# The opening of a two-layer backbone kernel, ordered by feature tiles

## Chip, cores and metric

The kernel runs on one core of a Trainium2 chip. The metric is the time of one execution on the device, in microseconds (us); for a kernel it is the median of several runs. A separate execution is recorded by the hardware profiler; from it come the page of the profile and the trace.

The engines of a core: TensorE (PE; its weight loads are shown apart as PEld) does the matrix products, VectorE (DVE) and ScalarE (ACT) work on whole tiles of 128 partitions, GpSimd (POOL) does some more of this, and SyncE (SP) issues transfers from the chip's main memory (DMA).

## The reference

Two layers over 512 latent tokens `x` (1024 features) and 256 context tokens `ctx`, all in float32. Every layer is a mixer and a SwiGLU feed-forward part (FFN), each behind an RMS norm whose result is scaled and shifted ("modulated") by six vectors per stream that are computed from a conditioning vector. Layer 0 mixes by windowed attention with 16 query heads and 4 heads of keys and values, layer 1 by retention. Cut to what bears on the change:

```python
c_act, cc_act = silu(c), silu(c_ctx)
for i in range(2):
    mx = split(c_act @ ada_w[i] + ada_b[i], 6)        # latent: shift, scale, gate, shift, scale, gate
    mc = split(cc_act @ ada_w[i] + ada_b[i], 6)       # context
    h_x = rms_norm(x, norm1_g[i]) * (1 + mx[1]) + mx[0]
    h_c = rms_norm(y_ctx, norm1_g[i]) * (1 + mc[1]) + mc[0]
    # layer 0
    q_x, k_x, v_x = split(h_x @ w_qkv, [1024, 1280])
    k_c, v_c = split(h_c @ w_qkv[:, 1024:], 2)
    q_x, k_x = rope_2d(rms_norm(q_x)), rope_2d(rms_norm(k_x))
    out_x = softmax([q k_c, q k_window, sink]) [v_c, v_window] @ w_o
    # layer 1: retention with decay log_g = log_sigmoid(ret_decay_logit)
    x = x + mx[2] * out_x                             # y_ctx likewise in layer 0
    x = x + mx[5] * swiglu(rms_norm(x) * (1 + mx[4]) + mx[3])
```

## The kernel before

**Layout and precision.** All activations stand with features on the partitions and tokens along the free axis: `x` is eight tiles (one for each 128 features) of 128x512, the context eight of 128x256. A float32 operand of a matrix product is split into a rounded high part and the remainder, and each product is three matmuls, high·high, low·high, high·low (`mm3`, L143). A weight tile of 128x1024 comes by a DMA, ScalarE makes its high part by a copy, VectorE its low part by a subtraction (`split`, L163, or in the opening `split_w` and `split_low`, L380 and L384).

**Order.** Each engine runs its own instructions strictly in order. In the opening that order is the program's own, written out by hand in a block (L469 to L518) for TensorE, VectorE and ScalarE; a second block (L635 to L652) holds TensorE's order up to the context's values, while a scheduler orders the other engines there. After it the scheduler orders all of them. All weights come through the queue of SyncE, in the order in which the program issues them; an issue whose buffer is still in use holds up those behind it. Pools with a fixed number of buffers of a name set how far ahead a load may be ("adan" has eight, "wraw" two).

**The opening**, in the order of its code:

- `load_stream` (L168) loads `x` in eight tiles. `add_square` (L205) squares each tile on ScalarE and adds it on VectorE to one list of sums, seven adds for eight tiles. `rms` (L216) sums this over the partitions by a matmul with a matrix of ones, and `neg_half_rstd` (L194) makes the inverse root from it in three ScalarE and two VectorE steps. `busy` (L415) are matmuls on the ones whose result is not used.
- The modulation of norm 1 is needed first. `ada_quarter` (L337) computes shift and scale for two feature tiles (a quarter of the eight), for both streams: 64 small TensorE instructions over four weight tiles, a copy of the row on ScalarE, two transposes on TensorE, and VectorE's `columns`, which add the bias and fold in the norm's gain. The four quarters' weights are `adaQ`.
- The rest of the modulation comes in units of four feature tiles (`ada_unit`, L309: 32 TensorE instructions, a copy on ScalarE, a transpose, an add of the bias). Four of them, `UNITS = (4, 5, 8, 6)` (L28), are in the opening. The first unit's weights stand in buffers that the keys use later ("k"), the three others' in "adan".
- `hidden0` (L430) makes the modulated rows of some feature tiles: the scaled row (VectorE, L438), the shifted high part (ScalarE, L439), the low part (VectorE).
- `keys(s, q)` (L445) and `values(s, q)` (L456) add what the two feature tiles of quarter q give to the keys and values of stream s (0 is the latent one), the keys by 12 matmuls for a quarter. Four weight tiles serve them: two for the keys (128 of the 256 columns each, all eight feature tiles), two for the values (all 256 columns, four feature tiles each). So all of the keys' weights have to be split before the first quarter is finished.

**Behind the opening.** `values(0, 2)` and the last unit's transpose and columns (`c1`), then `rope_key` and `key_factor` (norm and rotation of the keys), the query tile 0 in parts (`make_q`, L564; `q0[0]` to `q0[3]`) and the remaining values. Its second weight tile and the rest follow in the scheduler's order. `Block` (L675 on) is one query block of 128 tokens of the attention with its scores (L703), softmax and value products (L740). At L788 to L809 a chain of 24 small VectorE instructions turns the decay logits into the columns of retention's decay (`lg`, `dcol`); the scheduler has put it into VectorE's opening, partly between L199 and L358. The FFN of layer 0 computes 22 feature tiles `f`.

## Time and profile before

| | us |
|---|---|
| median of three runs | 1748.8 (1748.38, 1748.8, 1749.9) |
| the profiled execution's own time | 1746.2 |
| its span, first to last instruction | 1744.4 |
| mean granted TensorE clock, share of full speed | 0.999 |

TensorE's busy time in stretches of the span, in us:

| stretch | length | PE busy | DVE busy | ACT busy | DMA share |
|---|---|---|---|---|---|
| 0 to 20 | 20 | 10.99 | 12.37 | 12.22 | 0.92 |
| 20 to 50 | 30 | 27.75 | 22.61 | 13.87 | 0.96 |
| 50 to 80 | 30 | 28.02 | 15.33 | 13.05 | 0.64 |
| 80 to 130 | 50 | 46.81 | 45.51 | 37.67 | 0.04 |
| 130 to 225 | 95 | 93.43 | 71.30 | 64.06 | 0.09 |
| 318 to the end | 1426 | 1417.42 | 1110.67 | 640.86 | 0.38 |

How the views are read. A row of the *windows* gives a stretch, its length, the busy time and number of instructions of PE, PEld, DVE, ACT and POOL, then the granted clock, the share of time that the core's DMA engines were busy, and GB/s. A row of the *timeline* gives the start, the duration, the engine, the line of the kernel, the operation, what is written and read, its shape, how many instructions follow each other in this row (the duration is that of all of them), and in brackets the engine's idle time ahead of it with what released it. In the view of *DMA issues* stand the tile, the queue, the number, the size of each, and the median time from issue to landing.

### The profile page before, as it was taken

What the parts mean: (1) busy time and instruction counts of PE and PEld (TensorE: products, weight loads), DVE (VectorE), ACT (ScalarE), POOL (GpSimd) and SP (SyncE); (2) the same over time, 40 slices, a digit from 0 to 9 for tenths busy, and PEclk for the clock granted to TensorE, in tenths of its full rate; (3) what the DMA queues carried; (4) which work ended last, traced back from release to release, by engine and by line L of the source; (5) the groups of instructions that cost most, each with busy time, mean ns of one, the idle gap of its engine ahead of it and who ended that gap; (6) DMA issues with size and microseconds to landing.
All of it is one profiled execution on the core that took longest, in us unless ns stands there. A gap on an engine that the chain in (4) does not pass through costs nothing.

```text
span 1744.4 us, 27605 instructions
## 1 busy us (share of the span) xinstructions
PE 1712.7 (98%) x10876; PEld 1527.8 (88%) x10876; DVE 1350.5 (77%) x2368; ACT 846.3 (49%) x1492; POOL 131.0 (8%) x270
## 2 busy tenths in 40 slices
PE   7999999999999999999999999999999999999999
PEld 5777777899999999999988888898898899999997
DVE  6697778788778788787889858758768798777774
ACT  5576667465433334342456534525525565445442
POOL 0035435000000000000000000000000000000000
PEclk9999999999999999999999999999999999999999
DMA  9501012533243534343423524423423224233322
GB/s 353 230 13 38 13 43 68 204 122 135 71 147 121 158 109 145 123 153 101 156 99 86 182 84 130 162 86 121 157 85 118 76 84 132 77 117 101 104 79 85
DMA packets 59602, 203.54 MB, mean 117 GB/s; under 512 B 6608, under 2 KB 6992, under 8 KB 59216
## 3 DMA queue, kind: packets, MB, share of 16 engines
q1 hardware_dynamic: 51984, 175.03, 30.9%
q0 software_dynamic: 7200, 26.22, 5.2%
q8 instruction: 85, 1.39, 0.3%
q10 hardware_dynamic: 288, 0.52, 0.1%
q14 instruction: 45, 0.37, 0.1%
HBM read 199.65 MB, written 2.10 MB: 116 GB/s over the span
## 4 chain that ended last, share of the span: by engine, by line
PE 80%; DVE 8%; DMA 5%; ACT 3%; issue 2%; POOL 1%; SPq 0%; ACTq 0%; POOLq 0%; DVEq 0%
PE Y L886 15%; PE Z L886 7%; PE pj L147 6%; PE pj L148 6%; PE pj L149 6%; PE Z L1268 6%; PE X L886 4%; PE Y L1257 3%; PE pj L1268 2%; PE pT L726 2%; PE X L1257 2%; DMA wraw<-in_wst_dram 2%; PE pO L740 2%; PE S L703 2%; DMA adan<-in_adaQ_dram 1%
## 5 line engine op out<-in xcount | busy, mean ns | idle before, releaser
L164 ACT CAST whi<-wraw 128x1024 fp32r<-128x1024 f32 x258 | 270.2, 1051 | 370.7 <-PE Z L149 88.5
L165 DVE TENSOR_TENSOR wlo<-wraw,whi 128x1024 fp32r<-128x1024 f32 x258 | 315.0, 1223 | 60.9 <-ACT whi L164 59.7
L886 PE MATMUL Y<-aq,whi 128*128 128x384 f32 x640 | 173.7, 335 | 0.5 <-ACT sq L1044 0.5
L256 DVE SCALAR_TENSOR_TENSOR res<-pj,mod,res 128x512 f32<-128x512 f32 (+1 forms) x112 | 81.5, 729 | 65.6 <-PE pj L149 65.0
L886 PEld LDWEIGHTS Y<-aq,whi 128*128 128x128 f32 x640 | 116.6, 188 | 1.7 <-ACT sq L1044 0.9
L273 DVE CUSTOM_DVE_ANT_0 y<-adaw,crow,small_sb 128x1024 bf16<-128x1024 f32 x64 | 81.9, 1280 | 36.0 <-DMA adaw<-in_adaT_dram 35.7
L886 PE MATMUL Y<-aq,wlo 128*128 128x384 f32 x320 | 107.0, 334 | 0.0
L101 ACT ACTIVATE pr<-pr,stat,qs 128x513 f32<-128x513 f32 (+2 forms) x96 | 74.4, 777 | 23.5 <-DVE stat L710 22.9
L1268 PE MATMUL Z<-whi,sA 128*128 128x512 f32 x256 | 81.0, 391 | 1.2 <-ACT gate L1454 1.2
L717 POOL TENSOR_SCALAR pr<-pr,stat 128x512 f32<-128x512 f32 (+2 forms) x96 | 70.2, 744 | 79.5 <-DVE stat L714 54.8
L147 PE MATMUL pj<-ax,whi 128*128 128x512 f32 x176 | 68.8, 391 | 0.1
L149 PE MATMUL pj<-ax,whi 128*128 128x512 f32 x176 | 68.7, 390 | 0.0
L148 PE MATMUL pj<-ax,wlo 128*128 128x512 f32 x176 | 68.5, 389 | 0.0
L147 PE MATMUL pj<-act,whi 128*128 128x512 f32 x168 | 66.0, 393 | 0.0
L148 PE MATMUL pj<-act,wlo 128*128 128x512 f32 x168 | 65.9, 392 | 0.0
L149 PE MATMUL pj<-act,whi 128*128 128x512 f32 x168 | 65.5, 390 | 0.0
L270 POOL DMA_DIRECT2D adaw<-in_adaT_dram x48 | 25.6, 533 | 514.9 <-DVE mod L273 413.6
L726 PE MATMUL pT<-const_sb,pr 128*128 128x128 f32 x352 | 57.4, 285 | 6.1 <-POOL pr L717 3.6
L886 PE MATMUL Y<-sA,whi 128*128 128x256 f32 x304 | 60.6, 282 | 0.2 <-ACT res L1721 0.2
L886 PEld LDWEIGHTS Y<-aq,wlo 128*128 128x128 f32 x320 | 60.1, 188 | 0.0
L726 PEld LDWEIGHTS pT<-const_sb,pr 128*128 128x128 f32 x352 | 39.1, 142 | 23.0 <-POOL pr L717 12.4
L1268 PEld LDWEIGHTS Z<-whi,sA 128*128 128x128 f32 x256 | 48.0, 188 | 11.7 <-ACT gate L1454 1.9
(576 smaller groups left out, 5150.3 us busy)
## 6 DMA issues: line engine op xcount, KB each, us to landing
wraw<-in_wst_dram SPq DMA_DIRECT2D x224, 512.0 KB, 3.7
adaw<-in_adaT_dram POOLq DMA_DIRECT2D x48, 512.0 KB, 3.9
wx<-in_wst_dram SPq DMA_DIRECT2D x30, 512.0 KB, 4.3
adan<-in_adaQ_dram SPq DMA_DIRECT2D x16, 512.0 KB, 8.5
adan<-in_adaN_dram SPq DMA_DIRECT2D x12, 512.0 KB, 7.8
adaw<-in_adaT_dram SPq DMA_DIRECT2D x8, 512.0 KB, 3.9
res<-in_xT_dram SPq DMA_DIRECT2D x14, 256.0 KB, 3.8
aq<-in_adaN_dram SPq DMA_DIRECT2D x12, 256.0 KB, 5.8
```

The source lines that it names most:

```text
L101: ins = nc.scalar.activation(*args, **kw)
L147: nc.tensor.matmul(o, whi, xhi, start=first, stop=False)
L148: nc.tensor.matmul(o, wlo, xhi, start=False, stop=False)
L149: return nc.tensor.matmul(o, whi, xlo, start=False, stop=last)
L164: after(nc.scalar.copy(hi, t), behind)
L165: return nc.vector.tensor_tensor(lo, t, hi, op=sub)
L256: return nc.vector.scalar_tensor_tensor(res[d], o, mods[l, s][:, part, d:d + 1], res[d], mult, add)
L273: res.append(nc.vector.tensor_tensor_reduce(junk, w, cr[:, s * 1024:(s + 1) * 1024], 1.0, sm_t[:, C_ADAB + l * 48 + j:C_ADAB + l * 48 + j ...
L726: nc.tensor.transpose(tp[:, a * P:(a + 1) * P], self.pr[(0, 2, 1, 3)[a]][:, ki * P:(ki + 1) * P], ident)
L886: nc.tensor.matmul(o, p, r, start=first and k + i == 0, stop=k == 3 and i == 2, skip_group_check=not first)
L1257: ins = nc.tensor.matmul(o[:, e * SC:(e + 1) * SC], p[:, ws], r, start=first and k + e + i == 0, stop=k == 3 and i == 2, skip_group_check= ...
L1268: ins = nc.tensor.matmul(os[t], p, r, start=first and k + i == 0, stop=k == 3 and i == 2, skip_group_check=by_k or not first)
```

## The change

Everything is computed as before; the order, the grain and the places change.

- The sum of squares of `x` goes into two lists, alternately; `rms` adds both by two matmuls (`rest`).
- For quarters 0 and 1, `ada_tiles` replaces `ada_quarter`: for each of the two feature tiles 32 TensorE instructions, a copy, a transpose, the latent columns and the scaled row, one tile after the other; the context's columns come later. `adaQ[0:2]` is laid out accordingly.
- The weights of keys and values are four tiles by quarter: the two feature tiles' 256 key columns in the first half (`KEYS`), their value columns in the second (`VALUES`). High and low parts can be made by halves. `keys` can run part by part (high·high for all four pairs first).
- The context's squares and `rms(1)` come later, one quarter on.
- The modulation units come later: the first after the context's first values, the fourth after `q0[0]`. The loads are issued in a new order: the query tile 0's weights stand ahead of the second unit's, and the last unit, instead of the first, uses the "k" buffers. `values(0, 2)` comes ahead of the third unit.
- The decay chain becomes a function, called in layer 0's FFN at feature tile 12.
- Three fillers (`busy`) of five stand ahead of the sums.

```diff
@@ -213,11 +213,12 @@
...
         return ins
-    def rms(s, c=slice(None), bank=pj, behind=()):
+    def rms(s, c=slice(None), bank=pj, behind=(), rest=()):
...
         tot = bank()[:, :n]
-        after(nc.tensor.matmul(tot, ones, y, start=True, stop=True), behind)
+        for i, t in enumerate((y, *rest)):
+            after(nc.tensor.matmul(tot, ones, t, start=i == 0, stop=i == len(rest)), behind)
@@ -362,6 +363,35 @@
...
         return lambda: columns(1)
+    def ada_tiles(q, w, fill):
+        t = tv = None
+        bias = sm_t[:, C_ADAB:C_ADAB + 16].rearrange("p (f d) -> p f d", f=2)[:, :, 2 * q:2 * q + 2]
+        def columns(s, d0, d1):
+            col = mods[0, s][:, 0:2, 2 * q + d0:2 * q + d1]
+            nc.vector.tensor_tensor(col, tv[:, s, 0, :, d0:d1], bias[:, :, d0:d1], op=add)
+            nc.vector.tensor_tensor(col, tv[:, s, 1, :, d0:d1], col, op=add)
+            fold_gain(0, s, 0, 2 * q + d0, 2 * q + d1)
+        for d in range(2):
+            o = pT()[:, 0:P]
+            for k2 in range(4):
+                for j in range(4):
+                    k = 2 * k2 + j % 2
+                    nc.tensor.matmul(o[32 * j:32 * j + 32, :], ccol[:, k, :], w[2 * d + j // 2][:, k * P:(k + 1) * P],
+                                     start=k2 == 0, stop=k2 == 3)
+            rows = t_sq(P)
+            nc.scalar.copy(rows, o)
+            fill[d]()
+            if t is None:
+                t = pT()[:, 0:256]
+                tv = t.rearrange("p (d f h c) -> p c h f d", d=2, f=2, h=2)
+            nc.tensor.transpose(t[:, d * P:(d + 1) * P], rows, ident)
+            columns(0, d, d + 1)
+            scaled(2 * q + d)
+        return columns
@@ -377,36 +407,39 @@
...
         wpos[0] += 1
-    def split_w(pool):
-        wkv.append((T(pool, 1024, "whi", 2, F32R), T(pool, 1024, "wlo", 2, F32R)))
-        nc.scalar.copy(wkv[-1][0], raw[len(wkv) - 1])
-    def split_low():
-        i = lows.pop(0)
-        nc.vector.tensor_tensor(wkv[i][1], raw[i], wkv[i][0], op=sub)
-    lows = [0, 1, 2, 3]
+    KEYS, VALUES = slice(0, 512), slice(512, 1024)
+    def split_high(q, c=slice(0, 1024)):
+        if q == len(wkv):
+            pool = (st_p, rp)[q // 2]
+            wkv.append((T(pool, 1024, "whi", 2, F32R), T(pool, 1024, "wlo", 2, F32R)))
+        nc.scalar.copy(wkv[q][0][:, c], raw[q][:, c])
+    def split_low(q, c=slice(0, 1024)):
+        nc.vector.tensor_tensor(wkv[q][1][:, c], raw[q][:, c], wkv[q][0][:, c], op=sub)
...
     load_w(rp, "wraw", 2)
+    wq.append(ada_quarter_load(1))
     load_w(rp, "wraw", 2)
-    load_w(st_p, "adan", 8)
-    wq.append(ada_quarter_load(1))
     res0[1] = load_stream(1)
-    load_w(st_p, "adan", 8)
-    wq += [ada_quarter_load(2), ada_quarter_load(3)]
+    for q in (2, 3):
+        wq.append(ada_quarter_load(q))
+        load_w(rp, "wraw", 2)
...
         nc.sync.dma_start(mt, masks[:, 4 * i * P:4 * i * P + mt.shape[1]])
+    wu = [unit_load(UNITS[0])]
     q0_raw = w_raw()
-    first_unit = [T(akv, 512, "k", 8) for _ in range(KT)]
-    for k, t in enumerate(first_unit):
-        nc.sync.dma_start(t, adaN[UNITS[0], k // 2][:, k % 2 * 512:k % 2 * 512 + 512])
-    wu = [first_unit] + [unit_load(u) for u in UNITS[1:]]
+    wu += [unit_load(u) for u in UNITS[1:3]]
+    last_unit = [T(akv, 512, "k", 8) for _ in range(KT)]
+    for k, t in enumerate(last_unit):
+        nc.sync.dma_start(t, adaN[UNITS[3], k // 2][:, k % 2 * 512:k % 2 * 512 + 512])
+    wu.append(last_unit)
@@ -416,17 +449,38 @@
         nc.tensor.matmul(kvv[2][:, :n], ones, res0[0][0][:, :n], start=True, stop=True)
-    def squares0(s):
+    def squares1():
         for k in range(KT):
-            add_square(s, k, res0[s][k], tmp=(lambda n: T(st_p, 512, "hs", 3)[:, :n], lambda n: T(st_p, SC, "sc", 2)[:, :n])[s])
-    def stats0(s):
-        squares0(s)
+            add_square(1, k, res0[1][k], tmp=lambda n: T(st_p, SC, "sc", 2)[:, :n])
+    def stats0():
+        ssq[0] = t_y(0)
+        sums = ssq[0], t_sq(SX)
+        for k in range(KT):
+            sq = sums[k] if k < 2 else T(st_p, 512, "hs", 3)
+            nc.scalar.activation(sq, res0[0][k], AF.Square)
+            if k > 1:
+                nc.vector.tensor_tensor(sums[k % 2], sums[k % 2], sq, op=add)
...
         ln_exp_turn()
-        rms(s, bank=pT)
-    def hidden0(s, *ks, between=()):
+        rms(0, bank=pT, rest=sums[1:])
+    ts0 = {}
+    def scaled(k):
+        h[0].append(h_tiles(0))
+        ts0[k] = T(st_p, 512, "hs", 3)
+        nc.vector.scalar_tensor_tensor(ts0[k], res0[0][k], acol[0, 0, 0][:, k:k + 1], ssq[0], mult, mult)
+    def shift(k):
+        nc.scalar.activation(h[0][k][0], ts0[k], AF.Identity, bias=mods[0, 0][:, 0, k:k + 1])
+    def low(k):
+        nc.vector.scalar_tensor_tensor(h[0][k][1], ts0[k], mods[0, 0][:, 0, k:k + 1], h[0][k][0], add, sub)
+    def hidden0(s, *ks):
@@ -437,19 +491,20 @@
...
             nc.scalar.activation(h[s][k][0], ts[-1], AF.Identity, bias=mods[0, s][:, 0, k:k + 1])
-        for b in between:
-            b()
...
             nc.vector.scalar_tensor_tensor(h[s][k][1], t, mods[0, s][:, 0, k:k + 1], h[s][k][0], add, sub)
-    def keys(s, q):
-        for j in range(2):
+    def keys(s, q, by_part=False):
+        ks = (2 * q, 2 * q + 1)
+        order = ([(i, k, j) for i in range(3) for k in ks for j in range(2)] if by_part else
+                 [(i, k, j) for j in range(2) for i in range(3) for k in ks])
+        for i, k, j in order:
             o = kvx[j] if s == 0 else kvc[:, j * SC:(j + 1) * SC]
-            for i, (a, b) in enumerate(((0, 0), (1, 0), (0, 1))):
-                for k in (2 * q, 2 * q + 1):
-                    last = nc.tensor.matmul(o, wkv[j][a][:, k * P:(k + 1) * P], h[s][k][b],
-                                            start=k + i == 0 and (s == 0 or j == 0),
-                                            stop=k == KT - 1 and i == 2, skip_group_check=s == 1)
+            a, b = ((0, 0), (1, 0), (0, 1))[i]
+            c0 = (k % 2 * 2 + j) * P
+            last = nc.tensor.matmul(o, wkv[q][a][:, c0:c0 + P], h[s][k][b],
+                                    start=k + i == 0 and (s == 0 or j == 0),
+                                    stop=k == KT - 1 and i == 2, skip_group_check=s == 1)
@@ -458,8 +513,8 @@
...
             for k in (2 * q, 2 * q + 1):
-                cs = slice((k % 4) * 256, (k % 4) * 256 + 256)
-                (whi, wlo), (hi, lo) = wkv[2 + q // 2], h[s][k]
+                cs = slice(512 + k % 2 * 256, 768 + k % 2 * 256)
+                (whi, wlo), (hi, lo) = wkv[q], h[s][k]
@@ -467,54 +522,62 @@
         return first
     with tc.manual_schedule(engines={mybir.EngineType.PE, mybir.EngineType.DVE, mybir.EngineType.Activation}):
-        for n in (SX, SX, SX, SX, 256):
+        for n in (SX, SX, 256):
             busy(n)
-        stats0(0)
-        c1 = ada_quarter(0, wq[0], lambda: busy(256))
-        split_w(st_p)
+        stats0()
+        columns = ada_tiles(0, wq[0], [lambda: busy(256), lambda: (split_high(0, KEYS), shift(0), busy(256))])
+        shift(1)
         busy(SX)
-        hidden0(0, 0, 1, between=(split_low,))
-        c1()
-        split_w(st_p)
-        split_low()
-        keys(0, 0)
-        split_w(rp)
-        split_low()
-        squares0(1)
-        c1 = ada_quarter(1, wq[1], lambda: values(0, 0, (0, 1)))
-        hidden0(0, 2, 3)
-        c1()
-        values(0, 0, (2, 3))
-        rms(1, bank=pT)
-        keys(0, 1)
-        c1 = ada_quarter(2, wq[2], lambda: values(0, 1, (0, 1)))
+        split_high(0, VALUES)
+        split_low(0, KEYS)
+        for k in range(2):
+            low(k)
+        keys(0, 0, by_part=True)
+        columns(1, 0, 2)
+        split_low(0, VALUES)
+        values(0, 0, (0,))
+        columns = ada_tiles(1, wq[1], [lambda: (split_high(1, KEYS), values(0, 0, (1,))),
+                                       lambda: (shift(2), values(0, 0, (2,)))])
+        shift(3)
+        split_high(1, VALUES)
+        split_low(1, KEYS)
+        for k in range(2, 4):
+            low(k)
+        values(0, 0, (3,))
+        split_low(1, VALUES)
+        columns(1, 0, 2)
+        squares1()
+        keys(0, 1, by_part=True)
+        values(0, 1, (0, 1))
+        c1 = ada_quarter(2, wq[2], lambda: (rms(1, bank=pT), values(0, 1, (2,))))
         c1()
         hidden0(1, 0, 1)
-        split_w(rp)
+        split_high(2)
         hidden0(1, 2, 3)
-        values(0, 1, (2, 3))
+        values(0, 1, (3,))
         c1 = ada_quarter(3, wq[3], lambda: (keys(1, 0), hidden0(0, 4, 5)))
         c1()
-        split_low()
+        split_low(2)
         keys(1, 1)
         hidden0(0, 6, 7)
+        split_high(3)
         keys(0, 2)
-        c1 = ada_unit(UNITS[0], wu[0])
         hidden0(1, 4, 5)
         hidden0(1, 6, 7)
-        c1()
+        split_low(3)
         values(1, 0)
         values(1, 1)
-        c1 = ada_unit(UNITS[1], wu[1])
+        c1 = ada_unit(UNITS[0], wu[0])
         for i, mt in enumerate(mtmp):
             nc.vector.tensor_copy(mask[:, 4 * i * P:4 * i * P + mt.shape[1]], mt)
         keys(1, 2)
         c1()
+        keys(0, 3)
+        c1 = ada_unit(UNITS[1], wu[1])
+        keys(1, 3)
+        c1()
+        values(0, 2)
         c1 = ada_unit(UNITS[2], wu[2])
-        keys(0, 3)
-        last_key = keys(1, 3)
-        c1()
-        c1 = ada_unit(UNITS[3], wu[3])
     St.close()
     At = ExitStack()
     ap = At.enter_context(tc.tile_pool(name="ap", bufs=1, reuse_waits="tile"))
@@ -633,12 +696,13 @@
     q0 = make_q(0, q0_raw)
     with tc.manual_schedule(engines={mybir.EngineType.PE}):
-        after(values(0, 2), [last_key])
         c1()
         rope_key(kn[0])
         key_factor(0)
         q0[0]()
+        c1 = ada_unit(UNITS[3], wu[3])
         key_factor(1)
+        c1()
         for e in range(2):
             kx[e] = key_parts(e, kn[0])
         q0[1]()
@@ -791,22 +855,24 @@
...
     lnexp(t1, t1, AF.Exp, scale=-1.0)
-    nc.vector.tensor_scalar(t2, t1, 2.0, None, op0=add)
...
+    def decay(behind):
+        after(nc.vector.tensor_scalar(t2, t1, 2.0, None, op0=add), behind)
+        nc.vector.reciprocal(t2, t2)
...
+        nc.vector.tensor_scalar(dcol[:, 3, :], lg[:, 4:8], -1.0, None, op0=mult)
@@ -1141,6 +1207,8 @@
...
                     ada_next(end)
+                if f == 12:
+                    decay([end])
@@ -1783,10 +1851,10 @@
+    wk = qkv[:, 1024:1280].reshape(4, 2, P, 256).transpose(0, 2, 1, 3).reshape(4, P, 512)
+    wv = qkv[:, 1280:1536].reshape(4, 2, P, 256).transpose(0, 2, 1, 3).reshape(4, P, 512)
+    ch += [np.concatenate([wk[i], wv[i]], axis=1) for i in range(4)]
...
```

32 lines of the change are left out of this document (14 added, 18 removed).

## The prediction

> **What bounds it now.** First the page's head and busy times, then the windows view, which says stage by stage where TensorE loses time.
>
> ```profile
> span 1744.4 us, 27605 instructions
> PE 1712.7 (98%) x10876; PEld 1527.8 (88%) x10876; DVE 1350.5 (77%) x2368; ACT 846.3 (49%) x1492; POOL 131.0 (8%) x270
> ...
> 100.00:130.00 30.00, 26.81 (x178) 21.15 (x177) 28.47 (x83) 23.95 (x52) 11.40 (x24) 1.00 0.00 1
> ...
> 225.00:318.00 93.00, 88.32 (x643) 71.15 (x643) 72.69 (x233) 64.56 (x161) 37.63 (x79) 0.98 0.18 55
> ...
> 600.00:700.00 100.00, 100.00 (x577) 94.90 (x576) 78.00 (x117) 34.55 (x53) 6.33 (x12) 1.00 0.42 127
> ```
>
> After the window's own length come each engine's busy time and instructions. The kernel is TensorE: 98% busy, 100 of 100 us in a stretch of the first FFN. What can be won lies in the idle time: the opening, the start of the attention (100 to 130 us: 3.19 us idle, with VectorE 28.47 of 30 busy) and its end (225 to 318: 4.68). The instruction order of the changed kernel, set against the one before, shows that the projections' and attention's order changes up to about 225 us and is the same after it, but for small VectorE work in the first FFN. So what has been gained or lost at that point goes through to the end, and the 4.68 us stay.
>
> The opening itself I read in the timeline.
>
> ```profile
> 5.89 5.59 PE L417 MATMUL kvv<-res,ones_sb 128*128 128x512 f32 x10 [5.89 <-DMA res<-in_xT_dram]
> ...
> 6.32 2.80 ACT L212 ACTIVATE hs<-res 128x512 f32<-128x512 f32 x5
> ...
> 6.96 5.48 DVE L213 TENSOR_TENSOR y<-y,hs 128x512 f32<-128x512 f32 x7 [2.11 <-ACT hs L212]
> ...
> 12.50 1.12 PE L220 MATMUL pT<-y,ones_sb 128*128 128x512 f32 x2 [1.02 <-DVE y L213]
> ...
> 15.76 0.68 DVE L199 SCALAR_TENSOR_TENSOR sq<-pT,sq 128x512 f32<-128x512 f32 x1
> ...
> 16.47 0.69 DVE L200 SCALAR_TENSOR_TENSOR y<-sq,y 128x512 f32<-128x512 f32 x1
> ...
> 17.37 0.15 DVE L358 TENSOR_TENSOR mod<-pT,small_sb 128x4 f32<-128x4 f32 x1
> ...
> 17.95 1.41 DVE L438 SCALAR_TENSOR_TENSOR hs<-res,acol,y 128x512 f32<-128x512 f32 x2
> ...
> 19.28 1.22 DVE L386 TENSOR_TENSOR wlo<-wraw,whi 128x1024 fp32r<-128x1024 f32 x1
> 19.51 0.50 PE L450 MATMUL pj<-h,whi 128*128 128x512 f32 x1 [1.70 <-ACT h L439]
> ...
> 24.61 1.96 PE L345 MATMUL pT<-adan,ccol 128*32 128x128 f32 x64
> ```
>
> Columns are start, duration, instruction, count, and in brackets the idle time before it with its releaser. The first key product starts at 19.51, the first round of twelve has been issued at 24.61; in between TensorE waits on ScalarE and VectorE.
>
> **The change, part by part.**
>
> *The sum of squares in two lists.* Before, seven adds on one list take 5.48, 0.78 each. After, six adds alternate between two lists. The first needs the third square, at about 7.5 (squares come every 0.56, so one later than 6.96); at 0.69 each (a 128x512 add's own length) they end at 11.6 instead of 12.44. The list's own matmul with ones (some 0.5 of the 1.12) is new, but the first list's runs under the last add. Gain 0.8, bounds 0.3 and 1.3; I take 1.1, since two independent adds follow each other as closely as the pair in row L438 (1.41 for two).
>
> *Fillers.* Two of the five products on ones ahead of the sums go (L417, ten instructions in 5.59). TensorE waits there anyway: 0. If its clock were at half at 18 for want of them, the first twelve products would take up to 2.8 more, most of it under VectorE's work below.
>
> *The decay chain moved to the first FFN.* L804 and the four L806-809 go away between L199 and L358: L200 would follow L199 by 0.60 and L358 follow L200 by 0.60, 1.2 instead of 1.61. Gain 0.4. In the FFN the 24 small instructions of 0.15 to 0.2 each, some 4 us in all, go between larger ones; VectorE is 78% busy there and TensorE never idle, which hides them. Without that cover they cost up to 4 us. I take 0.
>
> *Split by quarter, columns and normalised row between transposes.* The first key product starts 1.5 earlier, at 18.0. From the first normalised row at 16.4 VectorE runs, one behind the other: row 0.7, columns 0.6 (L358 to L438), row 0.7, half a split 0.6 (half of 1.22), two low parts 0.7 each: 20.4. Four products follow, 0.35 each at worst: 21.8. Against 24.6 that is 2.8 gained.
>
> Now what VectorE does next, and the rest of the stretch as it was:
>
> ```profile
> 25.85 3.07 DVE L213 TENSOR_TENSOR y<-y,sc 128x256 f32<-128x256 f32 x6 [0.53 <-ACT sc L212]
> ...
> 30.34 0.59 PE L220 MATMUL pT<-y,ones_sb 128*128 128x256 f32 x2
> ...
> 33.62 0.42 DVE L200 SCALAR_TENSOR_TENSOR y<-sq,y 128x256 f32<-128x256 f32 x1
> ...
> 38.52 0.16 DVE L358 TENSOR_TENSOR mod<-pT,small_sb 128x4 f32<-128x4 f32 x1 [4.48 <-PE pT L352]
> ...
> 39.46 0.87 DVE L438 SCALAR_TENSOR_TENSOR hs<-res,acol,y 128x256 f32<-128x256 f32 x2
> ...
> 46.98 1.22 DVE L386 TENSOR_TENSOR wlo<-adan,whi 128x1024 fp32r<-128x1024 f32 x1
> 48.11 1.56 PE L315 MATMUL pT<-k,ccol 128*32 128x128 f32 x48
> ...
> 60.75 0.64 PE L315 MATMUL pT<-adan,ccol 128*32 128x128 f32 x16 [0.59 <-DMA adan<-in_adaN_dram]
> 61.32 0.73 PE L450 MATMUL pj<-h,whi 128*128 128x512 f32 x2
> ...
> 64.18 0.40 PE L450 MATMUL pO<-hc,whi 128*128 128x256 f32 x2
> ...
> 65.80 1.95 PE L315 MATMUL pT<-adan,ccol 128*32 128x128 f32 x64
> ```
>
> From 20.4: context columns 0.6, value half of the split 0.6; then a round for each tile of the second quarter (32 unit matmuls 0.95, copy and transpose 0.7, columns 0.6, row 0.7), the second half, its two low parts, the columns: VectorE reaches the context's squares at about 30.9, after TensorE has computed value tiles in the gaps. Seven adds at 0.51 make 3.6, matmul 0.6, three steps on ScalarE and two on VectorE at 0.45 to 0.5 make 2.4, the columns 0.9 (38.52 to 39.46): the context's rows start at 38.4, not 39.46. The lead has shrunk to 1.1, because the context's squares, which filled a wait before, now stand in VectorE's queue.
>
> *A new wait.* The keys of the third quarter were done when the unit at 48.11 began; they used weights split long before. Now they need `split_low(2)`, which stands on VectorE behind the context rows, the latent rows and the columns. VectorE's block from 39.46 to 46.98 keeps its length, so this split runs from 45.9 to 47.1, and ten of the twelve products wait for it. A round takes 2.86 (61.32 to 64.18), 0.24 a product: it ends at 49.5, 1.4 later than before. TensorE is idle for some 2.6 us. Queued behind them are the context's values, whose operands are ready. All of the lead has gone here.
>
> *Modulation units later.* From there to the end of the last unit before `q0[0]`, TensorE has three units (1.95 each), one latent round of keys (2.86), two of the context (half of it, 1.43 each), two of values (2.9 each, as 67.68 to 70.77 below) and 0.2 of transposes: 17.6, so 67.0, against 67.75 (65.80 + 1.95) before. The row at 60.75 shows one of the waits for unit weights that vanish; all in all 48.11 to 67.75 held 2 to 3 us of them beyond the same work and one unit more. The queue of loads: the weights of the first query tile now wait in SP's queue for `split_low(2)`, 47.1, and the second unit's four tiles stand behind them.
>
> ```profile
> 45.62 12.32 SPq L306 DMA_DIRECT2D adan<-in_adaN_dram  x12
> adan<-in_adaN_dram SPq DMA_DIRECT2D x12, 512.0 KB, 7.8
> ```
>
> At 7.8 us to the landing of the first and 1.03 a tile after it (12.32 for 12) they are there by 58, and needed at 58.6. Just hidden: 0, and up to 3 if not. The third unit is issued when the first's tiles are free (54.3) and needed at 65: hidden. The second quarter's tiles stand behind one weight tile, not three, so some 2 us earlier, and are needed 2.6 earlier: 0, up to 1 if not.
>
> *What hid the keys' work on ScalarE.* ScalarE works in order; its key work stands behind the copy of the last unit's row:
>
> ```profile
> 67.87 0.27 ACT L318 COPY sq<-pT 128x128 f32<-128x128 f32 x1 [6.09 <-PE pT L315]
> 67.68 0.39 PE L464 MATMUL kvv<-whi,h 128*128 128x256 f32 x1
> ...
> 70.77 1.02 PE L542 MATMUL pT<-pr,const_sb 128*128 128x512 f32 x2
> 71.90 0.50 PE L147 MATMUL pj<-h,pr 128*128 128x512 f32 x1
> ...
> 76.42 0.79 PE L147 MATMUL pj<-h,pr 128*128 128x512 f32 x1
> 88.76 0.40 PE L147 MATMUL pj<-h,whi 128*128 128x512 f32 x1
> ...
> 119.05 1.95 PE L740 MATMUL pO<-tt,v 128*64 128x256 f32 x16
> 92.68 1.22 DVE L165 TENSOR_TENSOR wlo<-wraw,whi 128x1024 fp32r<-128x1024 f32 x1
> ```
>
> Seven ScalarE steps lie between that copy and the first query weights: 67.87 to 71.90 is 4.03. Before, `values(0, 2)` (67.68 to 70.77) filled it. After, it comes ahead of the unit, so TensorE has only the key factor's matmul, and waits 3. With the copy at 67.0 the query tile starts at 71.05; the fourth unit (1.95) and 0.3 for its copy and transpose come before the second part, which started at 76.42 and now starts at 77.8: 1.4 late.
>
> The second query tile started at 88.76. In the order after, the first eight scores (2 us) and a key factor's matmul (1) stand ahead of it, and the low split of its weights stands on VectorE behind the first tile's queries, where the third tile's stood before, at 92.68; a little later now, 93.1 to 94.3. TensorE comes to it at 93.0 (88.76 + 1.4 + 3, less 0.2), waits 1.3 and is some 2.5 behind; but scores, softmax and one more weight split are ahead. VectorE is the bound there (28.47 of 30), and its list up to the first value product holds the same work but for small differences: that product comes at about 120 instead of 119.05. The new order has more query products between the pieces of the attention; of the 3.19 us idle I take 0.3 as filled behind that point: 0.7 late at the end, with bounds of -2.3 (all of it filled) and +2.5 (nothing caught up).
>
> **Sum**, against the profiled execution: 1744.4 + 0.7 = 1745.1 us of span; this execution took 1746.2 in all, 1.8 more, so 1746.9; the median of three runs, 1748.8, lies 2.6 above that execution. 1749.5.
>
> **Rivals.** (a) *The lead is kept.* If the wait at the third quarter's keys is not there (2.6) and the 3 us behind the last unit are filled, 5.6 us are saved: 1744. The change then does what its order of work asks for. For it: only VectorE's block from 39.46 holds these keys, and the idle 3.19 us can take up late work. Against it: both queues are in order.
>
> (b) *The clock drops in the new waits: slower.* The windows around the one stall of this size:
>
> ```profile
> 260.00:262.00 2.00, 1.48 (x7) 0.88 (x5) 2.00 (x15) 2.00 (x5) 0.70 (x2) 0.87 0.00 0
> 262.00:264.00 2.00, 2.00 (x9) 1.82 (x9) 1.45 (x8) 1.44 (x6) 2.00 (x3) 0.50 0.04 8
> 18.00:20.00 2.00, 0.49 (x1) 0.19 (x1) 2.00 (x3) 1.26 (x2) 0.00 (x0) 1.00 1.03 422
> ```
>
> The first number is time, the last but two the granted clock. With 1.48 of 2 busy the clock fell to 0.87 in the mean and then to 0.50. The new waits at 44.5 (2.6) and 67 to 71 (one matmul in 4 us) are emptier. If each brings 3.5 us at half the clock, that costs 1.75 each, 3.5 for both: 1753. It decides when both drops come. Against: from 18 to 20 TensorE was busy 0.49 of 2 and kept a clock of 1.00. [...]
>
> (c) *The loads fall behind.* SP's queue holds the second unit behind the query weights. Landing 4 us later, at 62, it leaves TensorE waiting 3.4 at 58.6: 1753. For it, there was no slack in the loads before (60.75); against, VectorE is late as well there.
>
> **How the numbers follow.** A change under 0.2% (3.5 us) can't be told from none. Forecast, within that: 0.42, own range 1746 to 1752.3. (a) 0.28, faster. (b) 0.24 and (c) 0.06, slower, together 0.30. The range for 8 in 10 goes from 1743.5 (lead kept, most of it) to 1755 (both drops and a part of the loads).
>
> **What would show it.** First key product near 18.0, first round over near 21.8; the context rows on VectorE near 38.4; third-quarter keys with a wait of 2 to 3 us released by `split_low`; last unit's copy near 67 with TensorE then idle about 3 us until the query tile; a wait of about 1 us on the second query tile's low weights; first value product within 1.5 of 119.05; no wait for unit weights; a single clock drop, near 261. It would be wrong if that first value product came 4 us earlier or later, or if the idle sums after 225 us differed from 4.68.

## The result, and the profile after

| | median, us | lowest to highest | runs |
|---|---|---|---|
| before | 1748.99 | 1747.45 to 1749.90 | 6 |
| changed | 1756.16 | 1753.27 to 1759.09 | 6 |

The changed kernel takes 1.0041 of the time before, with a 95% interval of 1.0030 to 1.0051: 7.2 us slower. The forecast was 1749.5, no measurable change, with a range up to 1755. The runs of the changed kernel also lie further apart (5.8 us against 2.5).

Four windows of the changed kernel, and under them the same four of the kernel before (stretch, length, busy time and instructions of PE, PEld, DVE, ACT and POOL, granted clock, DMA share, GB/s):

```profile
0.00:40.00 40.00, 31.05 (x353) 21.67 (x353) 22.11 (x62) 20.63 (x42) 0.64 (x9) 1.00 0.98 382
40.00:70.00 30.00, 26.45 (x317) 22.64 (x316) 15.31 (x37) 8.99 (x19) 0.11 (x1) 0.94 0.82 303
70.00:110.00 40.00, 34.78 (x248) 28.81 (x248) 31.19 (x60) 28.49 (x57) 6.56 (x6) 0.91 0.14 41
110.00:130.00 20.00, 19.52 (x128) 15.96 (x127) 16.90 (x50) 13.97 (x30) 7.57 (x18) 1.00 0.10 27
```

```profile
0.00:40.00 40.00, 29.09 (x295) 19.47 (x299) 25.75 (x76) 20.62 (x38) 0.64 (x9) 1.00 0.93 354
40.00:70.00 30.00, 28.00 (x440) 23.78 (x434) 15.61 (x40) 10.50 (x22) 0.11 (x1) 1.00 0.87 341
70.00:110.00 40.00, 38.72 (x236) 32.85 (x236) 35.46 (x70) 30.79 (x63) 7.43 (x13) 1.00 0.13 40
110.00:130.00 20.00, 17.75 (x129) 13.54 (x128) 19.01 (x60) 14.90 (x32) 8.17 (x15) 1.00 0.00 1
```

Up to 40 us TensorE gets more done than before (31.05 of 40 busy, not 29.09), as the change means it to. Then two columns turn: from 40 to 110 its idle time is 3.55 + 5.22 = 8.77 us instead of 2.00 + 1.28 = 3.28, and the clock's mean is 0.94 and 0.91 instead of 1.00. Over the first 130 us the idle time is 18.2 us against 16.4, that is 1.8 more in all: 5.5 more from 40 to 110, less 2.0 that the change gains ahead of 40 and 1.8 behind 110, where the changed kernel hasn't come as far in its work. What comes on top doesn't show as idle time: a busy TensorE at half the clock.

The timeline of the changed kernel, TensorE's rows and the few of VectorE and ScalarE that release them (start, duration, engine, line, operation, tiles, shape, count; in brackets the idle time ahead and its releaser):

```profile
18.18 0.73 PE L505 MATMUL pj<-h,whi 128*128 128x512 f32 x2
...
20.99 1.07 PE L505 MATMUL pj<-h,whi 128*128 128x512 f32 x4
...
38.70 0.88 DVE L492 SCALAR_TENSOR_TENSOR hs<-res,acol,y 128x256 f32<-128x256 f32 x2
...
46.22 1.22 DVE L419 TENSOR_TENSOR wlo<-wraw,whi 128x1024 fp32r<-128x1024 f32 x1
...
47.49 1.09 PE L505 MATMUL pj<-h,wlo 128*128 128x512 f32 x2 [2.36 <-DVE wlo L419]
48.38 1.91 PE L505 MATMUL pj<-h,whi 128*128 128x512 f32 x4
...
50.94 0.70 PE L505 MATMUL pj<-h,whi 128*128 128x512 f32 x2
...
60.77 1.95 PE L316 MATMUL pT<-adan,ccol 128*32 128x128 f32 x64
...
69.29 0.27 ACT L319 COPY sq<-pT 128x128 f32<-128x128 f32 x1 [6.18 <-PE pT L316]
...
73.32 0.50 PE L147 MATMUL pj<-h,pr 128*128 128x512 f32 x1 [2.08 <-ACT pr L164]
...
82.03 0.47 PE L147 MATMUL pj<-h,pr 128*128 128x512 f32 x1
...
96.79 0.51 PE L767 MATMUL S<-k,q 128*128 128x256 f32 x2 [1.73 <-ACT v L722]
...
98.07 1.22 DVE L165 TENSOR_TENSOR wlo<-wraw,whi 128x1024 fp32r<-128x1024 f32 x1
99.34 0.80 PE L148 MATMUL pj<-h,wlo 128*128 128x512 f32 x1 [0.98 <-DVE wlo L165]
...
126.02 1.95 PE L804 MATMUL pO<-tt,v 128*64 128x256 f32 x16
```

There are three new waits: 2.36 us for the low part of the third quarter's weights (47.49), 2.08 us for the query weights that ScalarE makes last (73.32), and 1.73 + 0.98 us at the first scores and the second query tile (96.79 and 99.34). Behind the waits products of the same shape take longer: four key products take 1.91 us from 48.38, and took 1.07 from 20.99. The same stretch by windows of 3.41 us, laid on the points at which the clock changes:

```profile
44.25:47.67 3.42, 0.90 (x3) 0.36 (x3) 3.28 (x10) 0.34 (x1) 0.00 (x0) 1.00 0.11 43
47.67:51.08 3.41, 3.41 (x9) 2.64 (x10) 3.28 (x6) 2.66 (x4) 0.00 (x0) 0.50 0.74 249
71.56:74.97 3.41, 1.33 (x5) 0.88 (x6) 2.17 (x5) 3.38 (x7) 0.00 (x0) 1.00 0.00 0
74.97:78.39 3.42, 3.42 (x10) 2.65 (x9) 3.42 (x7) 0.70 (x2) 0.00 (x0) 0.50 0.53 153
95.45:98.87 3.42, 1.57 (x10) 1.28 (x10) 3.22 (x10) 3.42 (x9) 0.71 (x1) 1.00 0.02 5
98.87:102.28 3.41, 2.94 (x7) 2.36 (x8) 3.41 (x8) 2.38 (x6) 0.58 (x2) 0.50 0.50 148
```

Each window in which TensorE was busy for 0.90, 1.33 and 1.57 us of 3.41 is followed by a window at a clock of 0.50. Half a clock over 3.41 us costs up to 1.7 us, three times 5.1. With the 1.8 us of idle time this makes 6.9, and the first value product comes at 126.02 instead of 119.05, 6.97 later. By these rows that is the 7.2 us between the medians; whether each of the three is worth its 1.7 is for the experiments to say, and they say that it is less. (The spans of the two profiled executions, 1754.5 and 1744.4, lie 10.1 us apart. The one of before was 2.8 us under its median. The 3.1 us by which the spans differ more than the first value products arise behind those, from no cause that is shown here.)

### The profile page after: what moved, and what is told of

The parts are those of the page before. It is cut to its first block, busy times and chain, and to the rows that moved or that the text cites. A ratio compares the mean times of both kernels' runs of the same rounds, so it can differ in the third digit from the quotient of the medians.

```text
span 1754.5 us, 27629 instructions
## 1 busy us (share of the span) xinstructions
PE 1718.7 (98%) x10876; PEld 1532.7 (87%) x10876; DVE 1348.6 (77%) x2375; ACT 846.8 (48%) x1496; POOL 131.8 (8%) x270
## 4 chain that ended last, share of the span: by engine, by line
PE 78%; DVE 11%; ACT 4%; DMA 4%; issue 2%; POOL 1%; ACTq 0%; SPq 0%; DVEq 0%; POOLq 0%
PE Y L952 13%; PE pj L147 7%; PE pj L148 7%; PE pj L149 6%; PE Z L952 6%; PE Z L1336 6%; PE X L952 3%; PE Y L1325 3%; DMA wraw<-in_wst_dram 2%; PE pj L1336 2%; DVE wlo L165 2%; PE X L1325 2%; PE pT L790 2%; PE pO L804 2%; PE S L767 1%
## 5 line engine op out<-in xcount | busy, mean ns | idle before, releaser
L768 DVE CUSTOM_DVE_ANT_0 pr<-S,mask,qs 128x256 f32<-128x256 f32 (+1 forms) x96 | 52.9, 566 | 9.4 <-PE S L767 8.5
L952 PE MATMUL Y<-hx,whi 128*128 128x256 f32 x304 | 57.9, 280 | 0.2 <-ACT res L1794 0.2
```

The lines of the kernel that those rows point to most:

```text
L952: nc.tensor.matmul(o, p, r, start=first and k + i == 0, stop=k == 3 and i == 2, skip_group_check=not first)
```

## The experiments

Two theories stood against each other at first. One: the loss is made of the waits and of the half clock behind each, so whatever covers a wait gains the wait and up to 1.7 us. The rival: the loss arises behind 90 us, in the attention's order on VectorE, so an earlier start is lost again. The kernel before was run beside each group, and the differences are taken to it:

| kernel | median, us | before beside it | difference |
|---|---|---|---|
| changed | 1756.16 | 1748.99 | +7.2 |
| first wait covered | 1750.81 | 1748.13 | +2.7 |
| second wait covered | 1750.83 | 1748.13 | +2.7 |
| both covered | 1748.57 | 1748.13 | +0.4 |
| fillers in both | 1753.60 | 1748.13 | +5.5 |
| both covered, load earlier | 1748.70 | 1748.00 | +0.7 |
| both covered, buffers freed | 1745.09 | 1748.00 | -2.9 |
| buffers freed alone | 1753.18 | 1748.00 | +5.2 |
| as the fastest, decay chain in the opening | 1745.11 | 1748.00 | -2.9 |
| changed, once more | 1755.94 | 1748.51 | +7.4 |
| fillers in both, once more | 1754.12 | 1748.51 | +5.6 |
| fillers in all three | 1754.11 | 1748.51 | +5.6 |

**Covering the first wait.** The third quarter's keys go behind the context's values, whose operands are ready.

```diff
-        keys(0, 2)
         hidden0(1, 4, 5)
...
         values(1, 1)
+        keys(0, 2)
         c1 = ada_unit(UNITS[0], wu[0])
```

> Theory (waits and clock): the changed kernel loses its 7 us in three new waits of TensorE, near 45, 71 and 95 us, each of which is followed by 3.4 us at half the clock. With the context's values ahead of the third quarter's keys the first wait is covered: no half clock near 48, the unit behind it starts 2.5 to 4.6 us earlier than 54.39, and the median falls from 1756.2 to about 1752.5. Rival (attention's order): the loss arises behind 90 us, in the order of scores and query products and on VectorE; then the earlier start is lost again and the median stays at 1755 to 1756.5. Rival (loads): unit weights are late, TensorE waits for them near 56, and the median is 1754 to 1756.

Measured: 1.0019 of before (1.0010 to 1.0028), 4.5 us less than the changed kernel by the table. The rows of TensorE at the first and the second wait, and the window behind the third:

```profile
47.55 0.73 PE L505 MATMUL pj<-h,wlo 128*128 128x512 f32 x2 [0.19 <-DVE wlo L419]
...
70.32 0.49 PE L147 MATMUL pj<-h,pr 128*128 128x512 f32 x1 [2.08 <-ACT pr L164]
```

```profile
95.75:102.58 6.83, 6.23 (x15) 4.93 (x16) 6.05 (x12) 4.56 (x9) 2.43 (x4) 0.50 0.51 152
```

The wait of 2.36 has shrunk to 0.19, and the query tile starts at 70.32 instead of 73.32, though its own wait of 2.08 is unchanged. The edit takes away 2.2 us of waiting and brings twice that in the median; a half clock of 1.7 makes 3.9 of it, and the interval is 1.6 us wide to either side. The profiled execution can't say more: there the third wait is followed by half a clock for two windows instead of one, and the first value product, at 124.56, is only 1.5 us earlier. The unit behind the first wait starts at 50.04 instead of 54.39; 0.71 us of this go to a new wait for the fourth quarter's low part (55.27). The units' weights didn't hold it up.

**Covering the second wait.** The values of the third quarter go back behind the unit, where they were.

```diff
-        values(0, 2)
         c1 = ada_unit(UNITS[2], wu[2])
+        values(0, 2)
```

> Theory (waits and clock): the third quarter's values behind the last unit cover ScalarE's key work as before; the query tile starts near 70.4 instead of 73.32, no half clock near 75, and the median falls to about 1751.7. The wait and the half clock near 48 stay. Rival (attention's order): median 1755 to 1756.5.

Measured: 1.0016 (1.0008 to 1.0025). TensorE's row at the second wait:

```profile
71.58 0.49 PE L147 MATMUL pj<-h,pr 128*128 128x512 f32 x1
```

The wait of 2.08 ahead of this row is gone, and again 4.5 us are gained. (The row starts only 1.7 us earlier than in the changed kernel, since in this execution the first key product, at 19.29, is 1.1 us later.)

**Both.**

> Theory (waits and clock): both covers together add up, 1746 to 1749; the wait near 95 and its half clock may stay. Rival (attention's order): 1754 or more, since the place of the loss is behind both.

Measured: 1.0005 (0.9996 to 1.0013), as fast as before. The covers bring 6.8 us together and 4.5 each alone, so they add up but for a quarter. This speaks against the rival. The third wait is still there, in this kernel's timeline and in the two windows behind it:

```profile
89.54 0.51 PE L767 MATMUL S<-k,q 128*128 128x256 f32 x2 [1.92 <-ACT v L722]
```

```profile
91.14:94.56 3.42, 2.46 (x6) 1.98 (x7) 3.42 (x8) 2.38 (x4) 1.07 (x2) 0.50 0.44 117
94.56:97.97 3.41, 3.41 (x10) 2.64 (x9) 2.62 (x5) 2.54 (x6) 1.72 (x2) 0.50 0.56 172
```

**The clock alone.** Two products on ones (four instructions in the trace) are put into each of the first two waits. The order of everything else is the same, and the waits end with the same releasers.

```diff
+    def filler(count):
+        o = pT()
+        for _ in range(count):
+            nc.tensor.matmul(o, ones, res0[0][0], start=True, stop=True)
...
+            if fill and (i, k, j) == (1, 2 * q, 0):
+                filler(fill)
...
-        keys(0, 2)
+        keys(0, 2, fill=2)
...
         key_factor(0)
+        filler(2)
         q0[0]()
```

> Two products on ones, whose result nobody reads, stand in each of the first two waits; nothing else differs. Theory (waits and clock): the waits end when they did, but the clock stays at 1.00 near 48 and 75, 1.7 us each: median about 1752.8. If the half clock has no part in the loss (the waits alone, or the order behind them): 1755.5 to 1756.5.

Measured: 1.0032 (1.0020 to 1.0045), 1.7 us less than the changed kernel by the table. Its timeline at the first wait, and three of its windows:

```profile
45.29 1.88 PE L455 MATMUL pT<-res,ones_sb 128*128 128x512 f32 x4
47.80 0.73 PE L512 MATMUL pj<-h,wlo 128*128 128x512 f32 x2 [0.63 <-DVE wlo L419]
```

```profile
48.79:52.21 3.42, 3.42 (x25) 3.14 (x24) 3.10 (x7) 2.90 (x5) 0.11 (x1) 1.00 0.94 326
72.69:76.10 3.41, 3.23 (x14) 2.55 (x14) 3.41 (x7) 1.68 (x3) 0.00 (x0) 1.00 0.29 67
96.58:99.99 3.41, 3.41 (x8) 2.75 (x9) 3.41 (x8) 2.38 (x5) 0.05 (x1) 0.50 0.52 154
```

No useful work was moved, and the clock stays at 1.00 behind both waits, while the third wait, which got no filler, is still followed by 0.50. The gain is about half of the 3.4 expected. So the changed kernel and the one with fillers were run again beside each other, with a third that has two more products on ones behind `values(1, 3)`:

> The changed kernel once more, unaltered, on the same chip as the two kernels with fillers, since the medians of before differ by 0.9 us between the measurements so far. 1.0035 to 1.0045 of before.

> The kernel with fillers in the first two waits, beside the unaltered one on the same chip. Theory (half clock, 1.7 us each): 2.6 to 3.4 us less than the changed kernel. If the half clock is worth less than the rows say, or is made good behind 130 us: less than 2.

> Two more products on ones behind the context's last values, ahead of the third wait; the scheduler then puts the first scores behind two query products, so this is not as clean as the two others. Theory: no half clock near 96, another 1.7 us less than with two fillers, 4.3 to 5.1 less than the changed kernel. Rival (two fillers already gave all that the clock is worth): the same as with two.

Measured, as ratios to before: 1.0038 (1.0025 to 1.0051), 1.0033 (1.0020 to 1.0045) and 1.0032 (1.0020 to 1.0045). The key product just ahead of the first wait and the first value product in the three, in this order, and for the last a window of all that lies between:

```profile
44.91 0.49 PE L505 MATMUL pj<-h,whi 128*128 128x512 f32 x1 [0.17 <-ACT h L493]
126.37 1.95 PE L804 MATMUL pO<-tt,v 128*64 128x256 f32 x16
```

```profile
44.48 0.50 PE L512 MATMUL pj<-h,whi 128*128 128x512 f32 x1 [0.17 <-ACT h L498]
122.84 1.95 PE L812 MATMUL pO<-tt,v 128*64 128x256 f32 x16
```

```profile
45.17 0.50 PE L512 MATMUL pj<-h,whi 128*128 128x512 f32 x1 [0.17 <-ACT h L498]
123.90 1.95 PE L813 MATMUL pO<-tt,v 128*64 128x256 f32 x16
```

```profile
44.00:130.00 86.00, 80.15 (x692) 65.12 (x692) 63.27 (x140) 50.26 (x102) 15.54 (x25) 1.00 0.31 113
```

From the one row to the other it is 81.46 us without fillers, 78.36 with two pairs, 78.73 with three. In the profiled executions the first two half clocks are thus worth 3.1 us, nearly the 3.4 of the rows. The medians say 1.8, which is the case "less than 2" of the expectation, and 1.7 in the first measurement; the intervals overlap, so between 1.7 and 3.1 nothing is settled. The third half clock shows no worth of its own: without it the value product comes no earlier (in an order that differs a little behind it). There the rival holds, in one place: behind 95 us something else than the clock sets the end. And with the clock at 1.00 from 44 to 130 us, three pairs of fillers leave the kernel 5.6 us slower than before and its first value product 4.9 us later (123.90 against 119.05). So more of the loss is the waits and what follows from them than the clock.

**Why the second query tile is late.** Its weights are loaded behind the last unit's eight tiles. One guess was that they come too late; the other, that they lie ready and find no buffer. Their high and low part go into the two buffers of "whi" and "wlo" in the pool `rp` (`w_parts`). Before, these held the two value weights, and the one of feature tiles 0 to 3 was done after the context's first values. After the split by quarter they hold quarters 2 and 3 (`pool = (st_p, rp)[q // 2]`), and both are in use to the end of the context's values. First the load alone, ahead of the last unit, on top of both covers:

```diff
     wu += [unit_load(u) for u in UNITS[1:3]]
+    q1_raw = w_raw()
...
-            w = next_w(ap, 0)
+            w = next_w(ap, 0, raw=ahead)
...
-    for piece in make_q(1):
+    for piece in make_q(1, ahead=q1_raw):
```

> Both covers of before, and the second query tile's weights are loaded ahead of the last unit's eight tiles; the order of TensorE, ScalarE and VectorE is the same. It is to say why the second query tile is late (the wait near 90 us, 1.92 and 1.00 us there, and the half clock behind it). Rival (load order): its weights stand too late in SyncE's queue; then their split comes earlier, the wait goes, and the median is about 1744.5. Theory (buffers): the low and high part of these weights need buffers that the fourth-quarter and third-quarter weights hold until the context's values are done; the loads have landed long before, and the median stays at 1748 to 1749.

Measured: 1.0004 (0.9995 to 1.0014); nothing gained. SyncE's and ScalarE's rows:

```profile
55.83 0.33 SPq L122 DMA_DIRECT2D wraw<-in_wst_dram  x1
...
90.40 1.09 ACT L164 CAST whi<-wraw 128x1024 fp32r<-128x1024 f32 x1
```

The load is issued at 55.83, and in the changed kernel this tile's loads take 3.5 to 10.0 us to land up to 110 us; the high part is made at 90.40, 34.6 us after the issue. It is not the load. Then the buffers: the context's values of quarter 2 follow the latent ones at once, so that this quarter's weights are done.

```diff
         c1 = ada_unit(UNITS[2], wu[2])
         values(0, 2)
+        values(1, 2)
...
         q0[3]()
-        values(1, 2)
         values(1, 3)
```

> Both covers, and the context's values of the third quarter stand behind the latent ones instead of at the end of the opening, so that the third quarter's weights are done early and their buffers free. Theory (buffers): ScalarE and VectorE split the second query tile's weights near 65 to 72 us as the kernel before did, its products follow the values without a wait, no half clock near 96; 3 to 4.4 us less than with both covers, median 1744 to 1746, faster than the kernel before. Rival (VectorE is the bound up to the first value product): the wait moves on, and the median stays at 1747.5 to 1749.

Measured: 0.9983 (0.9974 to 0.9992), 2.9 us faster than before. VectorE's and TensorE's rows, and a window:

```profile
71.95 1.21 DVE L165 TENSOR_TENSOR wlo<-wraw,whi 128x1024 fp32r<-128x1024 f32 x1
...
116.39 1.95 PE L804 MATMUL pO<-tt,v 128*64 128x256 f32 x16
```

```profile
96.00:100.00 4.00, 2.95 (x21) 2.56 (x20) 3.08 (x7) 3.90 (x10) 0.00 (x0) 1.00 0.01 2
```

The low part of these weights is made at 71.95, not at 98.07. In the kernel before it was:

```profile
73.09 1.22 DVE L165 TENSOR_TENSOR wlo<-wraw,whi 128x1024 fp32r<-128x1024 f32 x1
```

So the weights have their old place again; the clock is 1.00 in this window; the first value product comes at 116.39, 2.7 ahead of the kernel before. So what the change gains in its first 40 us can be kept to the end, if the three waits are gone.

**The buffers alone.** The changed kernel with `values(1, 2)` behind `values(0, 2)`, and neither of the covers.

> The changed kernel with the context's values of the third quarter behind the latent ones, nothing else. Theory: of the three half clocks near 48, 75 and 99 the third goes with its wait, 1.7 + 2.7 at most: median 1752 to 1753.5. Rival (VectorE is the bound): 1755 to 1756.5.

Measured: 1.0029 (1.0017 to 1.0041), 2.0 us less than the changed kernel. The second wait stays (2.09 us), and the third goes with its half clock, but another half clock comes later:

```profile
96.00:100.00 4.00, 3.81 (x17) 2.82 (x15) 3.81 (x8) 2.71 (x7) 0.00 (x0) 1.00 0.00 0
...
130.61:134.02 3.41, 3.41 (x14) 2.82 (x14) 3.11 (x13) 1.11 (x3) 0.70 (x4) 0.50 0.00 0
```

**The decay chain back in the opening**, on the fastest version: `decay` is called at its old place, and not at feature tile 12.

> The kernel with both covers and free buffers, and the decay chain back in the opening. Forecast's step (decay hidden in the FFN, gain 0.4 at the opening): 0 to 0.4 slower than the same kernel with the chain in the FFN. Rival (the 24 small instructions cost up to 4 us in the FFN): 1 to 4 faster.

Measured: 1745.11 against 1745.09, no difference that the runs can show (the intervals are 1.6 us wide to either side).

## Why the prediction was wrong, point by point

**The sum of squares: right.** 1.1 us were taken; the scaled row that opens the chain was to start at 16.4, and the first key product at 18.0. They started at 16.62 and 18.18. (The prediction's own sum gave a gain of 0.8 for the adds; they ended at 11.19 instead of 12.44.)

**The split by quarter: right.** First round over at 21.8, measured 20.99 + 1.07 = 22.06, where it had been 24.61. Context rows at 38.4, measured 38.70.

**The decay chain: not refuted, and too small to show.** It cost nothing that can be seen in the FFN. The gain of 0.4 in the opening can't be seen either: from the start of L199 to that of the scaled row it is 1.91 us on the fastest version, and 1.96 with the chain back in its place.

**The wait at the third quarter's keys: right in place, cause and size.** The split was to run from 45.9 to 47.1, and ran from 46.22; the wait was to be 2.6, and was 2.36. Its end was wrong: the round was to be over at 49.5 and was over at 50.94 + 0.70 = 51.64, since the products ran at half the clock from 47.67 to 51.08.

**The units: right.** No unit waited for its weights (the row at 60.77 has no wait); rival (c), loads that fall behind, didn't come. The last unit's copy was to start at 67.0 and started at 69.29, and 2.1 of this came with the late round.

**The key work on ScalarE: right to the digit.** From the copy to the query tile 4.03 us were carried over; 69.29 to 73.32 is 4.03. (The wait of 3 us came in pieces, of which 2.08 is the longest.) What followed was again the clock: the second part was to start at 77.8, and started at 82.03.

**The second query tile: mis-sized.** The prediction had a wait of 1.3 us for its low part, since "the low split of its weights stands on VectorE behind the first tile's queries". It is 0.98 there, but 1.73 ahead of it at the first scores, 2.71 together. The scores write accumulation banks that ScalarE's copies of the values free (the releaser in the row at 96.79), and the query products which covered these copies before were not ready. The cause, the buffers of the weights, was not seen at all: the change holds a weight tile longer than before, and this was to be read from the diff.

**The step that failed: the half clock left out of the sum, and behind it the size of the third wait.** The prediction put both waits in the right place, and then priced them as idle time alone. It had the drop as rival (b), at a chance of 0.24 and 3.5 us, and held against it that the clock stayed at 1.00 from 18 to 20 us. (Its 3.5 us at half the clock for each drop was an estimate; the windows show 3.41.) With 0.90, 1.33 and 1.57 us of work in 3.41 the next window was halved. The row at 260 had shown just this, a drop after a stretch with 1.48 of 2 us busy, and was the better evidence: the window ahead of that drop, 258.06 to 261.47, was busy for 2.02 us. The idle time from 18 to 20 us was shared by two windows, which were busy for 1.70 and 2.71 us. By the rows the sum with the clock in it is 1749.5, and 5.1 for three drops, and 1.4 for the third wait (2.71 less 1.3): 1756.0, and 1756.16 was measured. That they agree so closely is in part luck, since the experiments bear out the parts but not each size: a cover brings twice the wait that it covers (4.5 for 2.36 and for 2.08), fillers alone 1.7 to 3.1 for two drops and nothing for the third, and what lies behind 95 us goes with the late query tile (2.0 alone, 3.6 on top of both covers). By these the clock behind the first two waits is 1.7 to 3.1 of the 6.7 us by which the forecast missed, and the late query tile 2.0 to 3.6. What is left, up to 3.0, stays open.

**The likeliest case was the wrong one of the named.** Rival (b) was a part of the mechanism; its 1753 and the range's end at 1755 came from counting two waits, and the third was taken as 1.3 us that the attention would take up. The point that would make the forecast wrong was named and came: a first value product 4 us or more late. It was 6.97 late. The other sign held: from 225 to 318 us the idle time is 4.52, where it was 4.68. The single clock drop near 261 did not: there are four up to 318 us, the last from 269.53.

**Rival (a)**, that the lead is kept: not in this kernel. The version with all three waits gone shows that the change's own order of the first 40 us allows it.

## What to carry to other kernels

In the changed kernel three waits of TensorE that left 0.90, 1.33 and 1.57 us of a window of 3.41 us busy were each followed by half a clock. Beside the wait's own length that is up to 1.7 us more in the products behind it, and less where they would have waited anyway (fillers in two of the waits gained 1.7 to 3.1 us together): look up the granted clock in the windows behind every wait that a change makes, and cover the wait with work whose operands are ready, which may be work that stood later anyway. When weights are cut up in another way, list for each tile when its last reader comes, not only when its first: here each quarter's weights had keys and values in one tile, so two buffers were held until the end of the opening, and the weights that wanted them next were 25 us late without any row saying so. Where a change moves work ahead of a wait that it used to cover, its gain is given back at that very place.

## What the runs showed of the hardware

In these traces the half clock came on a grid. In the changed kernel the halved windows begin at 47.67, 74.97, 98.87 and 269.53 us; the distances are 27.30, 23.90 and 170.66, which is 8 times 3.413, 7 times 3.414 and 50 times 3.413. Carried back by this step, the grid has its first point at 3.29 us of the span in the changed kernel, and at 2.06 in the kernel before (from its halved window at 261.47). So it did not stand at the same place in the two executions. Further windows, each by its execution's own grid (first the changed kernel, then the kernel before):

```profile
266.12:269.53 3.41, 1.84 (x8) 1.08 (x7) 3.38 (x20) 3.03 (x7) 0.66 (x1) 1.00 0.02 5
269.53:272.95 3.42, 3.40 (x16) 3.19 (x15) 2.70 (x11) 2.76 (x11) 2.11 (x5) 0.50 0.00 0
```

```profile
15.71:19.13 3.42, 1.70 (x6) 0.50 (x5) 3.31 (x13) 1.68 (x3) 0.00 (x0) 1.00 1.03 422
19.13:22.54 3.41, 2.71 (x8) 1.34 (x8) 3.34 (x8) 2.88 (x4) 0.00 (x0) 1.00 1.02 417
```

In the changed kernel 1.84 us busy from 266.12 were followed by half a clock. The kernel before had 1.70 from 15.71 to 19.13 and kept its clock. In the traces of these two executions, laid on their grids from 10 us to the end, the windows at full clock with 0.00, 0.90, 0.98, 1.33 and 1.57 us busy were each followed by half a clock, and so were those with 1.84 and 2.02 us; those with 1.70, 2.00 and 2.20 us were not, and with 2.23 us or more none was. So in these two the border lies between 1.57 and 2.23 us and is not sharp in the busy time that the records give; what the chip counts stays open. Halved windows differed too in what followed: with both covers, the window from 91.14 was busy for 2.46 us at a clock of 0.50, and the next one was halved as well, 6.8 us for one wait. In the changed kernel the halved window from 98.87 was busy for 2.94 us, in the kernel before the one from 261.47 for 3.23 us, and the clock behind both was 1.00.

If the grid lies elsewhere in each run, as it did in these two executions, a wait of some 2 us could fall into one window in one run and be shared by two in another; this is an estimate from the two first points, 3.29 and 2.06. It would fit the wide spread of the changed kernel's runs, whose slowest (1759.09) had a mean clock of 0.994 and whose fastest (1753.27) one of 0.997; it is not shown, since in both profiled executions of this kernel the first two waits were followed by slow products (four key products behind the first took 1.91 us in both, from 48.38 and from 48.40, against 1.07 from 20.99; a query product behind the second took 0.63 us in both, from 75.76 and from 75.91, against 0.40 from 78.82).
